# The rope's product with exchanged halves in a hybrid encoder layer: one GpSimd instruction over 512 columns in place of two over 256

## The chip, the cores and the metric

The kernel runs on one core of a Trainium2 chip. The metric is the device time of one launch in microseconds (us), the median of several runs. Instructions go to five engines, each of which works through its own queue in order: TensorE (PE), VectorE (DVE), ScalarE (ACT), GpSimd (POOL) and SyncE (SP, which here issues nearly all DMAs). PEld is TensorE's weight load, which overlaps its products.

## What is computed

One encoder layer on 2048 + 512 tokens of width 1024. The input is normalised and multiplied by a 1024 x 9216 matrix. Some of the columns feed a neighbourhood attention, some feed three groups of dilated sliding-window attention (8 heads of 64 each), and the rest are gates. The change lies in the dilated part, where each query and key head is normalised and rotated:

```python
def rope(x):
    ...
    x1, x2 = xf[..., : dh // 2], xf[..., dh // 2:]
    return jnp.concatenate([x1 * cos - x2 * sin, x2 * cos + x1 * sin], axis=-1).astype(x.dtype)

    for gi, (win, dil) in enumerate(DIL_GROUPS):
        q = rope(rms_norm(heads(parts[base]), qn_b))
        k = rope(rms_norm(heads(parts[base + 1]), kn_b))
        o, lse = dilated_attention(q, k, heads(parts[base + 2]), win, dil)
```

So each output element is its own input times a cosine plus the input of the other half of its head times a signed sine.

## The kernel before, in words

The kernel has four stages, in this order: the dilated projections and attention (`dil_sweeps`, about 40 to 1220 us of the trace), the neighbourhood attention (`na_sweeps`, to about 1800 us), the gates (`gate_sweeps`) and the output product (`out_sweep`). Every value is kept as a sum of two fp16 numbers, "hi" and "lo", and a product is three matmuls.

In the dilated stage there are 60 tiles of 128 tokens (20 for each of the three groups), and each has three projection banks q, k and v of 512 columns: 24 matmuls into one of four PSUM banks named `proj`. For q and k, `dil_qk` (line 1407) does the rest, 120 times in all. ACT copies the bank into a buffer `qk` (there are three) and gives the bank back to PE, then squares it into `sq`; DVE sums the squares by head into `q_ssq`; POOL rotates (`rope`, lines 1433 to 1446): the product with the exchanged halves into `sq` (lines 1437 to 1439, two instructions, one for each half of the heads), the product with the own half in place (line 1441), and the sum of both (line 1442). Beside that, `rsqrt` (line 686) makes the 8 scales `q_y` of each row: two small ACT instructions, and five small POOL instructions on 8 columns (`q_c`, `q_t`, `q_y`). When both are there, POOL multiplies by `q_y` (`scale`, line 1448), ACT rounds to fp16 (`qs`, `high`), DVE or POOL makes the rest (`low`, line 1459), and SP issues the transposing DMAs. The factors `gcs` are made on POOL once for each tile (`rope_gains`, line 1389): for q and for k 64 cosines and 64 signed sines for each row, each times a gain.

The order of the instructions in each engine's queue is not left to the hardware or a compiler. The builder runs a clock of its own (`Clock`, line 112): each helper (`act`, `vec`, `pool`, `dma`) emits its instruction and adds a price to the time at which its engine is free; what follows is put on a heap at the time at which the clock says that the instruction is done, and is emitted when that time is reached. PE's matmuls are emitted as that clock goes on. `either` (line 384) puts an instruction on DVE or on POOL, whichever the clock says is done first. The prices of POOL and of that choice are:

```python
    def pool(self, ins, /, out, *a, n=None, **kw):
        getattr(self.nc.gpsimd, ins)(out, *a, **kw)
        self.clk.run("P", 0.23 + (n or size(out)) / 480)
...
        if self.clk.first(V=0.15 + n / 960 + PORT, P=0.23 + n / 480) == "V":
```

`size` counts the columns of one partition, and `PORT` is 0.18. The buffers (`Slots`) are given out by the same clock. An instruction emitted too early for its data holds up all that stands behind it on its engine.

Of the kernel before, what the change touches and what calls it, by code (L numbers as in the profile page):

```python
# [18 lines left out]
ALU = mybir.AluOpType  # L19
# [248 lines left out]
class Enc:  # L268
# [1138 lines left out]
    def dil_qk(self, R, i, ps):  # L1407

        clk, S, H = self.clk, self.S, R["H"]
        B = {}  # L1410

        def copy():
            B["x"] = self.new("qk", [128, 512])
            self.act(B["x"], ps)
            S["proj"].give(ps)
            S["sq"].take(square)

        def square():
            B["sq"] = self.new("sq", [128, 512])
            self.act(B["sq"], B["x"], AF.Square)  # L1420
            clk.then(reduce)

        def reduce():
            name = f"q{S['qk'].index(B['x'])}"
            ssq = self.T.tile([128, 8], F32, name=f"{name}_ssq", bufs=1)
            self.vec("tensor_reduce", ssq, B["sq"].rearrange("p (h d) -> p h d", d=64), axis=AX.X, op=ALU.add, n=512)
            both = B["both"] = Gate(clk, 2)
            both.when(scale)
            H["cs_gate"].when(rope)
            inv = self.inv["qk"[i], 2 + R["gi"]]  # L1430
            self.rsqrt(B, ssq, 8, QP ** 2 / 64, inv[:, 0:1], inv[:, 1:2], self.lnq, QS * QP, name, both.signal)

        def rope():
            x, sq, gcs = B["x"], B["sq"], H["gcs"]
            x4 = x.rearrange("p (h s e) -> p h s e", s=2, e=32)
            b4 = sq.rearrange("p (h s e) -> p h s e", s=2, e=32)
            for s in range(2):
                self.pool("tensor_tensor", b4[:, :, s], x4[:, :, 1 - s],
                          gcs[:, i, 1, 32 * s:32 * s + 32].unsqueeze(1).to_broadcast([128, 8, 32]), op=ALU.mult)
            x3 = x.rearrange("p (h d) -> p h d", d=64)  # L1440
            self.pool("tensor_tensor", x3, x3, gcs[:, i, 0].unsqueeze(1).to_broadcast([128, 8, 64]), op=ALU.mult)
            self.pool("tensor_tensor", x, x, sq, op=ALU.add)
            S["sq"].give(sq)
            if i == 1:
                S["cs"].give(H["cs"])
            B["both"].signal()

        def scale():
            x3 = B["x"].rearrange("p (h d) -> p h d", d=64)
            self.pool("tensor_tensor", x3, x3, B["y"].unsqueeze(2).to_broadcast([128, 8, 64]), op=ALU.mult)  # L1450
            clk.then(S["qs"].take, high)

        def high():
            B["qs"] = self.new("qs", [128, 1024], FP16)
            B["parts"] = self.parts(B["x"], B["qs"], 8)
            self.act(*B["parts"][0])
            clk.then(low)

        def low():
            self.either("tensor_tensor", *B["parts"][1], op=ALU.subtract)  # L1460
            S["qk"].give(B["x"])
            clk.then(R["place", i].when, turn)

        def turn():
            for out, rows in R["to", i]():
                self.turn(out, B["qs"][rows])
            S["qs"].give(B["qs"])
            R["ch"]["done"][R["i"]].signal()

        S["qk"].take(copy)  # L1470
# [744 lines left out]
```

## Time and profile before

| | |
|---|---|
| median of 3 runs | 2845.07 us (2841.5 to 2846.61) |
| the profiled execution's own time | 2850.0 us |
| its span, first to last instruction | 2847.9 us |
| PE busy | 2653.4 us (93%), 20853 instructions |
| DVE busy | 1612.5 us (57%) |
| ACT busy | 1365.8 us (48%) |
| POOL busy | 1460.0 us (51%) |
| the 16 DMA engines | mean 147 GB/s |

Busy time is the time in which an engine had an instruction under way. Matmuls are pipelined and their ends are modelled, so a busy PE is not PE at its peak; a gap of PE is a gap. PEclk is the clock that was granted to TensorE, as a part of full speed. A wait is put down to the instruction that ended last before it. In the rows, L356 is the helper of all matmuls, L360 that of the small transposes, L364 that of ACT, L369 that of DVE and L381 that of POOL, so instructions are told apart by the names of their tiles, output before inputs.

### The profile page before, as it was taken

To read this page: it belongs to the slowest core of one execution; us is meant where nothing else is said; L and a number is where in the kernel's file an instruction comes from. 1 tells how busy PE (TensorE), PEld (TensorE's weight loads), DVE (VectorE), ACT (ScalarE), POOL (GpSimd) and SP (SyncE) were. 2 spreads that over 40 slices of the span, in tenths; PEclk is the share of its full clock that TensorE was granted. 3 is DMA by queue.
4 is the path that set the end of the run, shared out by engine and by line. 5 is a ranking of instruction groups with operands and counts; after the bars stand their busy time and mean duration, and the time that the engine had idled before them with its cause. 6 is when DMAs were issued, how large, how long until landed. Compare 5 with 4: busy or idle time off the path is not lost. (4 is left out here: it accounts for less than half of the span.)

```text
span 2847.9 us, 55994 instructions
## 1 busy us (share of the span) xinstructions
PE 2653.4 (93%) x20853; PEld 1751.4 (61%) x20853; DVE 1612.5 (57%) x3716; ACT 1365.8 (48%) x3574; POOL 1460.0 (51%) x1996
## 2 busy tenths in 40 slices
PE   5998999989999999999899967799999999999999
PEld 2444444444444444455455544688888888888887
DVE  6787676785655765446686777432264544453111
ACT  5667666666666665656665667321132211222110
POOL 4887778777778898857665764100011221231110
PEclk9999999999999999999999975799999999999999
DMA  7898896776675765578998898431253444453443
GB/s 220 211 202 184 195 192 120 147 137 114 114 128 111 158 115 118 102 205 188 201 226 189 184 196 168 95 82 50 67 163 98 130 131 126 123 189 103 149 144 111
DMA packets 806721, 419.21 MB, mean 147 GB/s; under 512 B 688704, under 2 KB 733056, under 8 KB 800048
## 3 DMA queue, kind: packets, MB, share of 16 engines
q1 hardware_dynamic: 806016, 414.86, 63.4%
q8 instruction: 163, 2.67, 0.4%
q0 software_dynamic: 432, 0.77, 0.2%
q14 instruction: 110, 0.90, 0.1%
HBM read 171.72 MB, written 79.13 MB: 88 GB/s over the span
## 5 line engine op out<-in xcount | busy, mean ns | idle before, releaser
L356 PEld LDWEIGHTS <-hb 128*128 128x128 f16 x6240 | 590.3, 99 | 665.8 <-issue 109.2
L356 PE MATMUL proj<-wt,hb 128*128 128x512 f16 (+2 forms) x3420 | 691.4, 355 | 28.4 <-ACT qk L364 14.3
L356 PE MATMUL proj<-wu,hb 128*128 128x512 f16 x2880 | 663.3, 383 | 34.0 <-ACT qk L364 23.7
L356 PEld LDWEIGHTS <-wt 128*128 128x128 f16 x4560 | 445.8, 98 | 66.7 <-DMA hb<-htd 7.6
L364 ACT ACTIVATE sg<-proj,wi 128x256 f32<-128x256 f32 x240 | 113.0, 473 | 618.2 <-PE proj L356 615.6
L364 ACT ACTIVATE e<-e,neg,sc 128x256 f32<-128x256 f32 (+4 forms) x688 | 393.0, 572 | 5.1 <-DVE neg L369 2.9
L356 PE MATMUL proj<-hb,wt 128*128 128x256 f16 x2760 | 313.8, 273 | 9.8 <-DMA hb<-htd 7.4
L356 PEld LDWEIGHTS <-pT 128*128 128x128 f16 (+1 forms) x4560 | 227.4, 102 | 140.6 <-DMA pT<-p 65.3
L369 DVE TENSOR_TENSOR p<-e,p 128x512 f16<-128x512 f32 (+2 forms) x283 | 249.7, 883 | 65.6 <-ACT p L364 61.9
L381 POOL TENSOR_TENSOR sq<-qk,gcs 128x256 f32<-128x256 f32 x240 | 195.3, 834 | 164.3 <-DVE q_ssq L369 160.2
L381 POOL TENSOR_TENSOR qk<-qk,sq 128x512 f32<-128x512 f32 (+1 forms) x140 | 182.3, 1302 | 188.9 <-DVE qk L369 129.5
L369 DVE SCALAR_TENSOR_TENSOR qk<-s,binv,sg 128x256 f32<-128x256 f32 x160 | 77.1, 483 | 316.4 <-PE s L356 314.0
L356 PE MATMUL proj<-hb,kT 128*128 128x256 f16 x1920 | 227.5, 275 | 2.8 <-DVE kT L369 2.8
L381 POOL TENSOR_TENSOR hb<-sg,hb 128x256 f16<-128x256 f32 x66 | 53.4, 810 | 324.2 <-ACT hb L364 324.2
L356 PE MATMUL s<-hb,wt 128*128 128x256 f16 x1800 | 209.7, 273 | 2.2 <-DVE qk L369 2.1
L356 PEld LDWEIGHTS <-kT 128*128 128x128 f16 x1920 | 188.6, 99 | 26.6 <-DVE kT L369 3.1
L369 DVE CUSTOM_DVE_ANT_0 e<-s,cmask 128x256 f32<-128x256 f32 (+2 forms) x528 | 153.6, 344 | 64.5 <-PE s L356 53.7
L381 POOL TENSOR_TENSOR qk<-qk,q_y 128x512 f32<-128x512 f32 x160 | 177.4, 1113 | 4.8
L369 DVE CAST p<-e 128x512 f16<-128x512 f32 (+2 forms) x173 | 113.1, 654 | 108.1 <-ACT e L364 98.2
L369 DVE TENSOR_REDUCE q_ssq<-sq 128x8 f32<-128x512 f32 x160 | 108.8, 680 | 111.3 <-ACT sq L364 111.0
L381 POOL TENSOR_TENSOR qk<-qk,gcs 128x512 f32<-128x512 f32 x120 | 163.6, 1363 | 9.4
L369 DVE TENSOR_TENSOR qs<-qk,qs 128x512 f16<-128x512 f32 (+1 forms) x137 | 119.5, 874 | 79.3 <-ACT qs L364 77.0
(189 smaller groups left out, 3749.5 us busy)
## 6 DMA issues: line engine op xcount, KB each, us to landing
hb<-htd SPq DMA_DIRECT2D x40, 1024.0 KB
wr<-in_w_in SPq DMA_DIRECT2D x132, 256.0 KB
obd<-osb SPq DMA_DIRECT2D x50, 264.0 KB
hd<-xs SPq DMA_DIRECT2D x20, 512.0 KB
htd<-hb SPq DMA_DIRECT2D x10, 1024.0 KB
mad<-qk SPq DMA_DIRECT2D x40, 256.0 KB
e<-obd SPq DMA_DIRECT2D x40, 256.0 KB
sq<-mad SPq DMA_DIRECT2D x40, 256.0 KB
```

Of the source, the lines that this page charges most:

```text
L356: self.nc.tensor.matmul(out, a, b, start=start, stop=stop, **kw)
L364: self.nc.scalar.activation(out, x, func, **kw)
L369: getattr(self.nc.vector, ins)(out, *a, **kw)
L381: getattr(self.nc.gpsimd, ins)(out, *a, **kw)
```

## The change

Two instructions, each over 8 heads x 32 columns, become one over 8 heads x 2 halves x 32 columns. The input is read with the two halves of each head in reversed order, the sines are read as 64 columns repeated for 8 heads, and the output is written in order. What is multiplied with what, and where it is written, is the same. As `size(out)` is now 512, the builder's own price for this step is another one too.

```diff
@@ -1434,9 +1434,8 @@
             x, sq, gcs = B["x"], B["sq"], H["gcs"]
             x4 = x.rearrange("p (h s e) -> p h s e", s=2, e=32)
             b4 = sq.rearrange("p (h s e) -> p h s e", s=2, e=32)
-            for s in range(2):
-                self.pool("tensor_tensor", b4[:, :, s], x4[:, :, 1 - s],
-                          gcs[:, i, 1, 32 * s:32 * s + 32].unsqueeze(1).to_broadcast([128, 8, 32]), op=ALU.mult)
+            self.pool("tensor_tensor", b4, x4[:, :, ::-1], gcs[:, i, 1].rearrange("p (s e) -> p s e", s=2).unsqueeze(1)
+                      .to_broadcast([128, 8, 2, 32]), op=ALU.mult)
             x3 = x.rearrange("p (h d) -> p h d", d=64)
             self.pool("tensor_tensor", x3, x3, gcs[:, i, 0].unsqueeze(1).to_broadcast([128, 8, 64]), op=ALU.mult)
             self.pool("tensor_tensor", x, x, sq, op=ALU.add)
```

## Rows read from the trace of the kernel before

**Rows 1.** Busy time by stretch: us, then PE, PEld, DVE, ACT, POOL, clock, DMA.
```profile
40.00:400.00 360.00, 324.86 (x2252) 156.89 (x2251) 269.05 (x566) 238.92 (x603) 283.66 (x381) 0.98 0.86 194
400.00:800.00 400.00, 370.22 (x2835) 182.83 (x2834) 275.29 (x676) 258.35 (x723) 310.31 (x423) 0.98 0.71 132
800.00:1220.00 420.00, 410.71 (x3046) 202.61 (x3044) 244.85 (x693) 271.79 (x814) 352.84 (x501) 1.00 0.64 125
1220.00:1640.00 420.00, 393.65 (x3217) 225.80 (x3218) 284.13 (x676) 261.87 (x691) 271.59 (x434) 0.98 0.90 197
1640.00:1800.00 160.00, 105.88 (x1065) 68.74 (x1064) 117.98 (x291) 108.32 (x274) 78.46 (x81) 0.65 0.88 178
1800.00:2848.00 1048.00, 1036.82 (x8407) 909.67 (x8404) 397.41 (x749) 204.69 (x430) 154.25 (x160) 1.00 0.39 117
```

**Rows 2.** Waits, 40 to 1220 us: us in total, times, longest us.
```profile
PE proj L356 <- ACT qk L364: 40.5, 34, 3.2
...
PE proj L360 <- ACT qk L364: 4.2, 2, 2.2
...
ACT neg L364 <- DVE osb L369: 174.5, 137, 5.4
ACT qs L364 <- POOL qk L381: 75.2, 45, 6.9
...
POOL sq L381 <- DVE q_ssq L369: 160.2, 60, 17.2
```

**Rows 3.** Timeline of PE and ACT around two stalls: start, us, instruction, idle before.
```profile
175.27 0.63 ACT L364 ACTIVATE qs<-qk 128x512 f16<-128x512 f32 x1 [3.06 <-POOL qk L381]
175.81 0.58 ACT L364 ACTIVATE qk<-proj 128x512 f32<-128x512 f32 x1
176.44 0.81 PE L356 MATMUL proj<-wu,hb 128*128 128x512 f16 x3 [3.22 <-ACT qk L364]
...
825.17 0.63 ACT L364 ACTIVATE qs<-qk 128x512 f16<-128x512 f32 x1 [0.49 <-POOL qk L381]
...
831.00 3.40 PE L356 MATMUL proj<-wt,hb 128*128 128x512 f16 x15 [0.84 <-ACT qk L364]
```

**Rows 4.** POOL groups by shape, whole span: count, busy us, mean ns, idle before.
```profile
L381 POOL TENSOR_TENSOR sq<-qk,gcs 128x256 f32<-128x256 f32 x240 | 195.3, 834 | 164.3 <-DVE q_ssq L369 160.2 <-DVE x_c L369 1.8 <-DVE x_t L369 1.4
...
L381 POOL TENSOR_TENSOR qk<-qk,gcs 128x512 f32<-128x512 f32 x120 | 163.6, 1363 | 9.4
...
L381 POOL TENSOR_TENSOR bm<-G,namask 128x512 f32<-128x512 f32 x48 | 59.4, 1243 | 27.6 <-DVE mx L369 27.4
```

**Rows 5.** Tile gcs: count, duration ns min/median/max.
```profile
L381 POOL TENSOR_TENSOR sq<-qk,gcs x240: 710/727/1715, 44.3 to 1216.7; 128x256 f32<-128x256 f32 x120
L381 POOL TENSOR_TENSOR qk<-qk,gcs x120: 1263/1272/2134, 45.8 to 1217.5; 128x512 f32<-128x512 f32 x120
```

**Rows 6.** Timeline of POOL, one rope with nothing beside it.
```profile
717.11 1.40 POOL L381 TENSOR_TENSOR sq<-qk,gcs 128x256 f32<-128x256 f32 x2
718.59 1.27 POOL L381 TENSOR_TENSOR qk<-qk,gcs 128x512 f32<-128x512 f32 x1
719.94 1.26 POOL L381 TENSOR_TENSOR qk<-qk,sq 128x512 f32<-128x512 f32 x1
```

**Rows 7.** DVE and POOL groups by shape, 40 to 1220 us: count, busy us, mean ns.
```profile
L369 DVE TENSOR_TENSOR p<-e,p 128x512 f16<-128x512 f32 x146 | 137.6, 943 | 23.2 <-ACT p L364 20.8
L369 DVE TENSOR_TENSOR qs<-qk,qs 128x512 f16<-128x512 f32 x91 | 92.6, 1020 | 68.9 <-ACT qs L364 66.8
...
L369 DVE CAST p<-e 128x512 f16<-128x512 f32 x119 | 85.9, 723 | 77.5 <-ACT e L364 77.1
...
L381 POOL TENSOR_TENSOR qs<-qk,qs 128x512 f16<-128x512 f32 x27 | 34.4, 1276 | 9.8 <-ACT qs L364 9.8
...
L381 POOL TENSOR_TENSOR p<-e,p 128x512 f16<-128x512 f32 x18 | 23.5, 1304 | 9.9 <-DVE p L369 6.0 <-ACT p L364 3.9
```

**Rows 8.** Timeline of POOL and DVE from 382 us, and one undisturbed DVE subtraction.
```profile
382.18 1.27 POOL L381 TENSOR_TENSOR qk<-qk,gcs 128x512 f32<-128x512 f32 x1
383.53 1.59 POOL L381 TENSOR_TENSOR qk<-qk,sq 128x512 f32<-128x512 f32 x1
...
383.09 0.91 DVE L369 TENSOR_TENSOR p<-e,p 128x512 f16<-128x512 f32 x1 [0.88 <-ACT p L364]
...
716.39 0.69 DVE L369 TENSOR_TENSOR qs<-qk,qs 128x512 f16<-128x512 f32 x1 [0.38 <-ACT qs L364]
```

## The prediction, made before the changed kernel was run

> **What bounds the kernel now.** I read the busy times by stretch first [rows 1]. All ropes lie between 40 and 1220 us. PE is busy there for 324.9 + 370.2 + 410.7 = 1105.8 of 1180 us: it leaves 74 us idle, 35 and 30 of them before 800 us and 9 after it. POOL is the next fullest engine, 946.8 us or 80%, and 84% after 800 us, where PE hardly waits: a full POOL alone does not stop PE. After 1800 us PE is busy for 1037 of 1048 us and no rope is left. So a shorter rope can win at most what PE loses in the first 1220 us, and the waits say what that is [rows 2]: 36 stalls of 44.7 us in all, in which PE wants a projection bank that ACT has not yet copied out. The question is why ACT is late. Its copies stand in one queue with everything else, and ahead of them ACT waited for POOL's scaled `qk` 45 times, 75.2 us, and for DVE's maxima 137 times, 174.5 us [rows 2].
>
> The link can be seen whole [rows 3]. At 175.27 us ACT's rounding `qs` starts after 3.06 us of waiting for POOL's `qk`; the copy stands behind it and starts at 175.81; PE goes on at 176.44 after a stall of 3.22. I went through the 36 stalls in this way. In 11 of them ACT had waited for POOL in the 8 us before PE went on; they hold 16.4 us, the first being this one and the last the one at 831.00 (0.84 us, after a wait of 0.49). The other 25, 28.3 us, stand behind a wait for DVE, for a transfer, or behind ACT's own work.
>
> **The instruction itself.** The edit takes out 240 instructions of 256 columns and puts in 120 of 512. No row shows the new form. In the means two halves cost 2 x 834 = 1668 ns [rows 4]. The nearest row is the next instruction of the same rope: same buffers, same repeated factor, 512 columns, 1363 ns [rows 4]. The reversed read alone doesn't argue for more: the neighbourhood bias reads a tile in reversed order both ways at 1243 ns for 512 columns [rows 4]. I take 1363, so 305 ns a rope, 120 x 0.305 = **36.6 us** of POOL's time. The ends are far apart. By the medians it is 2 x 727 - 1272 = 182 ns or 21.8 us [rows 5]. Where nothing disturbs POOL, the step from the first half to the next instruction is 718.59 - 717.11 = 1.48 us and that of a 512 is 719.94 - 718.59 = 1.35 [rows 6]: only 0.13 a rope, 15.6 us. And as a pattern of three steps, one of them backward, is in no row, it may run as slowly as two halves, so nothing at all, or somewhat more. I take the mean and not the quiet value because the stalls happen where POOL is crowded; the excess over the median is 107 ns for each half but 91 for a 512 [rows 4, 5], as if it were paid by the instruction.
>
> **What of that reaches PE.** Of the 120 ropes 60 began on an idle POOL, which had waited for DVE's sums [rows 2]; there the saving only shortens the way of that tile, and the scale waits for ACT's `q_y` as well. Where POOL has fallen behind, one or two ropes lie between the late start and the `qk` that ACT waits for, so each of the 11 stalls shrinks by 0.31 to 0.61 us: 3.4 to 6.7 us. I take **5 us**; the ends are 0 (quiet value, hidden by the next wait) and 16.4 us (all 11 go). The next thing late is then ACT's wait for DVE, which the edit doesn't touch. In the stages behind 1220 us the edit has no instruction: 0.
>
> **The plan.** The builder prices a rope's first step at 2 x (0.23 + 256/480) = 1.53 us before and 0.23 + 512/480 = 1.30 after, 0.23 less, 27.6 us over 120. All that follows in its clock moves, so instructions change places in all five queues, SP's transposes too, and `either` finds POOL free sooner: by that, up to 27.6/1.297 = 21 more subtractions can pass from DVE (`qs` at 1020 ns) to POOL (1276) [rows 7], which gives back all that POOL won and takes some 21 us from DVE. I cost this at zero in the sum, as neither sign has a row for it, and give it its own cases below.
>
> **The sum.** 2850.0 - 5 = 2845 for the profiled execution, which stood 4.9 above the median; against the median of 2845.07 that is **2840**.
>
> **A rule that speaks against it.** DVE and POOL do hold each other up here. A DVE subtraction of 512 columns takes 0.69 us undisturbed; the one issued at 383.09, while POOL's product of 382.18 to 383.45 ran, took 0.91, and POOL's next, issued at 383.53, took 1.59 where 1.26 is usual [rows 6, 8]. Either waits for the other's whole instruction. The Trainium skill (SBUF — State Buffer, "Who interferes with whom") calls it an exclusive lock of the shared ports, held for the whole instruction, by GpSimd or by a VectorE instruction with two inputs in SBUF or in a two-port mode; by that rule a merged product shuts VectorE out for longer than each half did. Priced from rows: the halves hold 120 x 2 x 0.71 = 170 us, 14% of the stage. Of the 356 `p`, `qs` and cast instructions [rows 7] some 51 arrive in them and wait 0.36 on average; in a merged one they would wait 0.64. That is 51 x 0.28, **14 us more of waiting on DVE** (an estimate).
>
> **The rivals.** (a) *That lock decides.* DVE's maxima and roundings come later, ACT waits longer for them, and PE with it: the 25 other stalls grow. If all 14 us reached PE, the sum would be 2840 + 14 = **2854**. It decides from some 11 us on, as 5 are won elsewhere. For it: 174.5 us of ACT's waiting is for DVE. Against: DVE is idle for 25% of the time before 400 us and 31% from there to 800 [rows 1], and POOL, with fewer instructions, is shut out less often itself.
> (b) *The new order is worse.* Place: ACT's queue before 800 us. Its `qs` is put 0.23 us earlier, and an undisturbed chip delivers only 0.13; the rounding stands ahead of a bank's copy before its data are there, as at 175.27. A stall costs 44.7/36 = 1.24 us [rows 2], so ten more cost 12.4: **2852**. It decides from nine or ten more stalls on.
> (c) *The new order is better.* The same price with the other sign, ten stalls fewer: **2828**.
> (d) *The edit doesn't do what it says on the chip*: the merged instruction takes as long as two halves (1668), or the saving is covered by the waits for DVE's sums and for `q_y`: **2845**.
>
> **How the numbers follow.** The forecast (2833 to 2845) has 0.45; (a) 0.10, (b) 0.20, (c) 0.16, (d) 0.09. The spread of the three runs is 0.18%, so 0.2%, 5.7 us, is about what a measurement of this kernel can tell from no change: faster means below 2839.4, slower above 2850.8. The forecast lies at that bound and gives 0.24 to faster and 0.21 to the same. With (c) faster is 0.40; with (d) the same is 0.30; (a) and (b) make slower 0.30. The range goes from somewhat below (c) to somewhat above (a), 2824 to 2858: all the cases stand in it, and beyond it are larger changes of the order, for which I keep 0.2. As both signs hold much of the chance: the likeliest case's own range is 2833 to 2845.
>
> **What would show it.** Right: 120 instructions `sq<-qk,gcs` of 512 columns at a mean near 1363 ns and a minimum near 1263; POOL busy some 37 us less before 1220 us, unless POOL has more `qs` and `p` subtractions than the 27 and 18 of before [rows 7]; ACT's wait for POOL's `qk` below 75 us; PE's wait for ACT's copies near 40; the dilated stage ending about 5 us sooner, and the stages behind it as long as before. Wrong: a mean near 1668 is (d). DVE's `p` and `qs` with means up by 40 ns or more and more waiting of ACT for DVE is (a). A time that moves by over 10 us with most of the difference in stalls at new places, or behind 1220 us where no rope is, is the order, (b) or (c); it would mean that the price in the plan counts for more than the instruction.

## The result, and the profile after

The changed kernel takes 2873.93 us, median of 3 runs (2872.27 to 2874.89), against 2845.07: a ratio of 1.0103 with a 95% interval of 1.008 to 1.0126. It is slower by 29 us, three times what the worst of the rivals gave (2854) and outside the range.

First where the time went. The busy times by stretch of both kernels, cut 6 us after the start of ACT's last copy of a dilated bank (columns as in [rows 1]); the kernel before:

```profile
40.50:1216.30 1175.80, 1105.28 (x8128) 542.07 (x8126) 787.26 (x1925) 765.43 (x2126) 943.26 (x1300) 0.99 0.73 147
1216.30:2847.90 1631.60, 1536.35 (x12684) 1204.20 (x12684) 800.94 (x1723) 578.03 (x1407) 507.85 (x678) 0.96 0.57 144
```

The kernel after:

```profile
40.60:1240.60 1200.00, 1114.86 (x8115) 545.58 (x8113) 797.45 (x1940) 762.81 (x2118) 923.76 (x1181) 0.98 0.71 144
1240.60:2870.50 1629.90, 1535.63 (x12696) 1203.92 (x12696) 798.35 (x1724) 577.13 (x1403) 502.47 (x672) 0.96 0.57 144
```

The dilated stage is 24.2 us longer, the rest 1.7 us shorter. POOL is busy for 19.5 us less in the longer stage, so it got the relief that was meant. PE is idle for 85.1 us instead of 70.5, 14.6 more, and the same matmuls keep it busy for 9.6 us longer, at a granted clock of 0.98 where it was 0.99.

The instruction does what it says. From the tile view of `gcs` after (count, ns min/median/max), to be read against [rows 5]:

```profile
L381 POOL TENSOR_TENSOR sq<-qk,gcs x120: 1260/1272/2852, 44.4 to 1238.2; 128x512 f32<-128x512 f32 x120
L381 POOL TENSOR_TENSOR qk<-qk,gcs x120: 1265/1278/2339, 45.8 to 1239.5; 128x512 f32<-128x512 f32 x120
```

The reversed pattern costs nothing: its median of 1272 ns is no more than its neighbour's 1278. And the waits after, from 40.6 to 1240.6 us (us in total, times, longest), which answer to [rows 2]:

```profile
PE proj L356 <- ACT qk L364: 47.2, 36, 3.3
PE proj L356 <- DVE dv L369: 9.6, 7, 3.6
PE proj L360 <- DVE dv L369: 4.7, 1, 4.7
...
PE o L356 <- DMA pT<-p: 3.9, 4, 1.4
...
PE proj L360 <- ACT qk L364: 2.6, 2, 2.0
...
ACT neg L364 <- DVE osb L369: 203.4, 142, 9.3
...
ACT qs L364 <- POOL qk L381: 97.0, 48, 7.0
```

The same waits of PE for DVE and for transposes in the kernel before, from 40.5 to 1216.3 us:

```profile
PE proj L356 <- DVE wm L369: 7.3, 5, 1.9
PE proj L356 <- DVE dv L369: 6.3, 4, 3.4
...
PE o L356 <- DMA pT<-p: 0.9, 3, 0.4
```

POOL has less to do, and yet ACT waits longer for its `qk`: 97.0 us instead of 75.2, and 203.4 instead of 174.5 for DVE's maxima. PE's stalls behind ACT's copies have grown by 5.1 us (44.7 to 49.8), those behind DVE's `dv` by 8.0 (6.3 to 14.3), and those behind the transposes of `p` by 3.0. No single engine explains this; it looks like other instructions in front, which the experiments below test. The longest of these waits, in the timeline of the kernel after:

```profile
419.31 5.11 DVE L369 SCALAR_TENSOR_TENSOR wv<-wr,gf,wv 128x512 f16<-128x512 f32 x3
...
424.95 1.26 DVE L369 TENSOR_REDUCE wm<-wr 128x1 f32<-128x512 f32 x2
...
427.42 0.69 DVE L369 TENSOR_REDUCE wm<-wr 128x1 f32<-128x512 f32 x1 [1.21 <-DMA wr<-in_w_in]
...
428.78 0.69 DVE L369 SCALAR_TENSOR_TENSOR dv<-proj,dv 128x512 f16<-128x512 f32 x1 [0.28 <-issue]
429.53 0.37 PE L360 MATMUL proj<-ident,wm 128*1 128x128 f32 x1 [4.75 <-DVE dv L369]
...
432.41 0.30 ACT L364 ACTIVATE neg<-osb,sc 128x2 f32<-128x2 f32 x1 [9.29 <-DVE osb L369]
```

DVE's queue has work on the weights of the next group (`wv`, `wm`), one piece of it waiting for its load, ahead of `dv`, the instruction that gives a bank back. PE stands for 4.75 us, the scores behind it come late, and ACT, with a softmax's `neg` at the head of its queue, for 9.29 (the profile puts the last 1.4 us before DVE's maxima down to a transfer). The clock falls with it, by the windows of the kernel after:

```profile
420.00:440.00 20.00, 12.96 (x114) 6.88 (x113) 14.01 (x33) 9.87 (x25) 10.48 (x13) 0.74 0.77 163
```

PE was busy for 13 of these 20 us, at 0.74 of full speed in the mean, that is, for part of them at the lower of its two levels (1.2 instead of 2.4 GHz). So a stall is paid a second time in the clock.

The delay does not come evenly. Counted by ACT's copies of banks (`qk` and `dv` from `proj`), the kernel after loses 11.1 us on the one before between the 51st copy and the 62nd (394 to 484 us of its trace, where the place above lies), 6.2 us from there to the 111th, and 11.7 us between the 111th and the 131st; outside these it wins 4.8. Each of the three groups of tiles has 60 banks, so the two short stretches lie around the changes from group to group. The second of them, before and after, and in it PE's stalls behind `dv` after (before there are none):

```profile
816.90:939.10 122.20, 120.69 (x937) 60.39 (x936) 68.45 (x200) 80.00 (x239) 100.34 (x148) 1.00 0.66 123
```

```profile
831.50:965.40 133.90, 124.37 (x943) 61.40 (x942) 78.14 (x208) 82.96 (x248) 96.34 (x132) 0.99 0.65 122
```

```profile
PE proj L356 <- DVE dv L369: 5.3, 2, 3.6
```

### The profile page after: what moved, and what is told of

The parts are those of the page before. It is cut to its first block, busy times and chain, and to the rows that moved or that the text cites. A ratio compares the mean times of both kernels' runs of the same rounds, so it can differ in the third digit from the quotient of the medians.

```text
span 2870.5 us, 55899 instructions
## 1 busy us (share of the span) xinstructions
PE 2662.3 (93%) x20853; PEld 1754.6 (61%) x20853; DVE 1620.0 (56%) x3733; ACT 1362.2 (47%) x3562; POOL 1435.1 (50%) x1871
## 5 line engine op out<-in xcount | busy, mean ns | idle before, releaser
L381 POOL TENSOR_TENSOR sq<-qk,gcs 128x512 f32<-128x512 f32 x120 | 170.7, 1422 | 188.3 <-DVE q_ssq L369 182.1
L369 DVE TENSOR_TENSOR qs<-qk,qs 128x512 f16<-128x512 f32 (+1 forms) x147 | 136.2, 929 | 90.0 <-ACT qs L364 82.9
L381 POOL TENSOR_TENSOR qk<-qk,gcs 128x512 f32<-128x512 f32 x120 | 171.3, 1427 | 9.4
```

The source lines that it names most:

```text
L369: getattr(self.nc.vector, ins)(out, *a, **kw)
```

## The experiments

Two theories. **A**: the time is lost in the order of the queues, which the builder's clock makes from the price, and the instruction itself wins a little or nothing. **B**: the longer instruction shuts DVE out, and that makes the kernel slower. The edit changes an instruction and its price at once; two kernels take them apart.

**m_old**: the one instruction, with the order of before.

```diff
-            self.pool("tensor_tensor", b4, x4[:, :, ::-1], gcs[:, i, 1].rearrange("p (s e) -> p s e", s=2).unsqueeze(1)
+            self.nc.gpsimd.tensor_tensor(b4, x4[:, :, ::-1], gcs[:, i, 1].rearrange("p (s e) -> p s e", s=2).unsqueeze(1)
                       .to_broadcast([128, 8, 2, 32]), op=ALU.mult)
+            for _ in range(2):
+                clk.run("P", 0.23 + 256 / 480)
```

> One instruction over 512 columns, but charged in the builder's clock as the two halves were (2 x 0.763 us), so that every engine's queue has the order of the kernel before, instruction for instruction. Theory A (the new order lost the time, the instruction itself wins a little): 2838 to 2844 us, POOL's sq<-qk,gcs near 1.37 to 1.42 us, PE's stalls behind ACT's copies at or below the 44.7 us of before. Theory B (the longer instruction shuts DVE out and delays ACT): 2855 to 2875 us, with DVE's p and qs means up by 40 ns or more.

Measured: 2845.63 us against 2845.77 in the same session, ratio 1.0002 (0.9993 to 1.0012). Neither theory's number: the loss is gone, so B falls, but nothing is won. POOL and DVE groups of m_old, 40 to 1220 us (columns as in [rows 4, 7]), POOL first:

```profile
L381 POOL TENSOR_TENSOR qk<-qk,gcs 128x512 f32<-128x512 f32 x120 | 167.6, 1397 | 9.4
L1437 POOL TENSOR_TENSOR sq<-qk,gcs 128x512 f32<-128x512 f32 x120 | 165.7, 1381 | 179.6 <-DVE q_ssq L369 175.4 <-DVE x_c L369 1.8 <-DVE x_t L369 1.5
...
L369 DVE TENSOR_TENSOR p<-e,p 128x512 f16<-128x512 f32 x146 | 141.0, 966 | 22.3 <-ACT p L364 19.8
L369 DVE TENSOR_TENSOR qs<-qk,qs 128x512 f16<-128x512 f32 x91 | 97.3, 1071 | 63.5 <-ACT qs L364 61.5
```

As all queues stand as before, these compare row by row: the step takes 165.7 us in place of 195.3, so 29.6 are won; its neighbour is 34 ns slower; DVE's `p` is 23 ns and its `qs` 51 ns slower, 146 x 0.023 + 91 x 0.051 = 8 us on DVE. And the waits of m_old, 40 to 1220 us:

```profile
PE proj L356 <- ACT qk L364: 39.5, 33, 4.5
...
PE proj L360 <- ACT qk L364: 4.0, 2, 2.2
...
ACT neg L364 <- DVE osb L369: 184.2, 136, 5.4
...
ACT qs L364 <- POOL qk L381: 67.8, 40, 6.7
```

ACT waits 7.4 us less for POOL and 9.7 us more for DVE; PE's stalls behind ACT's copies go from 44.7 to 43.5. And POOL itself waits 15.2 us longer for DVE's sums, 175.4 us where it was 160.2. So nothing that POOL won reached PE; the trace shows these two ways in which it went, and not how much each counted.

**h_new**: the two halves, with the order of the changed kernel.

```diff
             for s in range(2):
-                self.pool("tensor_tensor", b4[:, :, s], x4[:, :, 1 - s],
+                self.nc.gpsimd.tensor_tensor(b4[:, :, s], x4[:, :, 1 - s],
                           gcs[:, i, 1, 32 * s:32 * s + 32].unsqueeze(1).to_broadcast([128, 8, 32]), op=ALU.mult)
+            clk.run("P", 0.23 + 512 / 480)
```

> Two instructions over 256 columns, charged as the one over 512 (0.23 + 512/480 = 1.297 us in all), so that every queue has the order of the changed kernel. Theory A: as slow as the changed kernel or a few us slower, 2872 to 2882 us. Theory B: about the kernel before, 2842 to 2850 us.

Measured: 2882.21 us, ratio 1.0124 (1.0109 to 1.014). The work is that of the kernel before, two halves included; only the places of instructions in the queues differ, and for some of those that the builder may put on either of two engines, the engine. And 36 us are lost. So A is shown: the order loses the time. In the traces m_old has the sequence of the kernel before and h_new that of the kernel after, instruction by instruction on every engine. In the new order the one instruction is worth some 6 to 8 us (2873.9 against 2882.2; the ratios are 0.0021 apart, 6 us, and their intervals overlap).

Why that order is bad was the next question: because POOL's step is priced too low (*price*), or because it is another order (*luck*)? **h_tick** is the kernel before with each half charged 0.001 us more, **m_mid** the one instruction charged 1.41:

```diff
+                clk.run("P", 0.23 + 256 / 480 + 1e-3)
...
+            clk.run("P", 1.41)
```

> The kernel before with each half charged 0.001 us more in the builder's clock and nothing else: the instructions are the same, but their order differs from about the tenth rope on. Theory A, in its strong form (any change of the order moves the time, by luck): a time that differs from 2845 by more than 6 us either way, between 2830 and 2875. Theory A in its weak form (the lower price makes roundings stand too early): within 5 us of 2845, as 0.002 us a rope puts nothing noticeably earlier. Theory B: within 5 us of 2845.

> One instruction over 512 columns, charged 1.41 us, midway between the 1.527 of the two halves and the 1.297 of the change, and near what it takes on the chip in the mean (1.42). Weak form of theory A: between the two, about 2855 us. Strong form: unrelated to the price, anywhere from 2830 to 2880. Theory B: about 2870, as the changed kernel.

Measured: h_tick 2845.47 us (1.0, 0.9986 to 1.0013), m_mid 2863.04 (1.006, 1.0044 to 1.0076). Both spoke for *price*: another order at the same price costs nothing, and half the cut costs about half.

Four more with the one instruction: charged 1.307 (**m_tick_up**), 1.293 (**m_tick_down**), 1.65 (**m_high**), and as in the change, with 0.23 put on a later step (**m_scale**):

```diff
             self.pool("tensor_tensor", x3, x3, B["y"].unsqueeze(2).to_broadcast([128, 8, 64]), op=ALU.mult)
+            clk.run("P", 0.23)
             clk.then(S["qs"].take, high)
```

> The changed kernel with its one instruction charged 0.01 us more (1.307 instead of 1.297); the order is the changed kernel's up to about 300 us of the run and another one after it. If the price is what counts (a POOL step that is charged too little puts ACT's roundings too early): 2868 to 2878 us, as the changed kernel. If it is luck (each order is a draw of its own): a time that differs from 2874 by more than 8 us, most probably below it, 2840 to 2866.

> The changed kernel with its one instruction charged 0.004 us less (1.293); the order is the changed kernel's up to about 560 us and another one after it. Price: 2868 to 2878 us. Luck: differs from 2874 by more than 8 us, but keeps what the changed kernel had lost by 560 us, about 4 us: 2848 to 2866.

> One instruction over 512 columns charged 1.65 us, 0.12 more than the two halves were. Price: roundings stand later than in the kernel before, so 2835 to 2846 us. Luck: anywhere from 2840 to 2880.

> The changed kernel, with the product by the scale, the last POOL step of each tile's query and key, charged 0.23 us more, so that POOL's work for one rope has the total that it was charged before, at another place. Price: back to 2840 to 2850 us. Luck: anywhere from 2840 to 2880.

Measured: 2871.72 us (1.0088), 2880.6 (1.012), 2851.06 (1.0013, 1.0001 to 1.0026) and **2837.33** (0.9967, 0.9955 to 0.9979). This looked like *price* once more, though the higher price didn't win. m_scale beats both kernels.

Then m_scale was taken apart: **m_later** plans only the rounding 0.23 us later, **m_full** only keeps POOL busy longer, **m_scale2** puts 0.46 in place of 0.23, and **h_scale** has m_scale's order with the two halves.

```diff
-            clk.then(S["qs"].take, high)
+            clk.at(clk.done + 0.23, S["qs"].take, high)
...
             clk.then(S["qs"].take, high)
+            clk.run("P", 0.23)
```

> The changed kernel, with the rounding that follows the scale planned 0.23 us later, while POOL counts as free as early as in the changed kernel. If what hurts is that roundings stand too early in ACT's queue: back to 2837 to 2850 us. If what hurts is that POOL's own queue is planned too full: 2865 to 2880 us, as the changed kernel.

> The changed kernel, with POOL counted as busy for 0.23 us after the scale, while the rounding is planned as early as in the changed kernel. Roundings too early: 2865 to 2880 us. POOL's queue too full: 2837 to 2850 us.

> As the version with the scale charged 0.23 us more (2837.3 us), but 0.46 more. If a more careful price goes on winning: 2828 to 2836 us. If 0.23 had already met what the chip takes, or its last 8 us were the luck of one order: 2838 to 2855 us, as the version with the instruction charged 1.65 us (2851).

> The order of the version with the scale charged 0.23 us more, instruction for instruction, but with the two halves in place of the one instruction. If the instruction itself is worth what it was in the changed kernel's order (2882.2 against 2873.9): 2843 to 2848 us. If it is worth nothing once the order is a good one, as it was in the order of before: 2835 to 2840 us.

Measured: m_later 2878.57 us (1.011), m_full 2863.61 (1.0063), m_scale2 2840.48 (0.9976, 0.9966 to 0.9987), h_scale 2842.63 (0.9988, 0.9979 to 0.9997). Neither part brings m_scale's time, and neither reading of "too early" or "too full" holds alone. The instruction is worth 5 to 6 us in this order (2837.3 against 2842.6; the ratios are 0.0021 apart too, and the two intervals just touch). As the kernels of either pair were measured in different sessions, neither worth is sure to a few us.

So there are three pairs with one order (in the traces h_scale has the sequence of m_scale on every engine too). ACT's waits in the two others, halves first, from 40.5 us to the end of the stage, cut as above; h_new (to be read against the kernel after), then h_scale and m_scale:

```profile
ACT neg L364 <- DVE osb L369: 197.1, 138, 8.1
...
ACT qs L364 <- POOL qk L381: 114.3, 53, 7.3
```

```profile
ACT neg L364 <- DVE osb L369: 174.7, 131, 6.4
...
ACT qs L364 <- POOL qk L381: 94.1, 45, 6.9
```

```profile
ACT neg L364 <- DVE osb L369: 181.0, 133, 6.4
...
ACT qs L364 <- POOL qk L381: 79.5, 43, 6.7
```

With the one instruction ACT waits longer for DVE in all three orders (9.7, 6.3 and 6.3 us) and shorter for POOL (7.4, 17.3 and 14.6 us). Where the second outweighs the first, the instruction wins 5 to 8 us; in the order of before it doesn't, and nothing is won. Each of these is one trace, so that is a sign and no proof.

The last six were to say whether the price counts at all: the low price in one group of tiles alone (**m_g0**, **m_g1**, **m_g2**), and in all groups at 1.07, 1.18 and 1.06 (**m_low**, **m_118**, **m_106**).

```diff
+            clk.run("P", 0.23 + 512 / 480 if R["gi"] == 0 else 2 * (0.23 + 256 / 480))
...
+            clk.run("P", 1.07)
```

> One instruction over 512 columns, charged 1.297 us in the first of the three groups of dilated tiles and 1.527 in the other two. If every rope that is charged too little costs its share (36 us over 120 with the halves, 29 with the one instruction): about 10 us over 2845, so 2852 to 2860. If one stage makes the loss: 2842 to 2850 unless it is this one. By the changed kernel's trace, which is 3.5 us behind at the end of this group: 2846 to 2851.

> The same with 1.297 us in the second group alone. Each its share: 2852 to 2860 us. One stage: by the changed kernel's trace this group lost 15.6 us, so 2858 to 2864.

> The same with 1.297 us in the third group alone. Each its share: 2852 to 2860 us. One stage: the changed kernel's trace lost 5 us in this group, so 2848 to 2853.

> One instruction, charged 1.07 us in all three groups, 0.23 less than the change charges. If the price goes on to count: 2885 to 2910 us. If the loss is a step that the change has already taken: 2865 to 2885 us. If it was luck: 2840 to 2865.

> One instruction charged 1.18 us, between the change's 1.297 (2874 us) and 1.07 (2849). If each price gives an order of its own with a time that the price does not foretell: anywhere from 2837 to 2882, most probably 2845 to 2870. If the loss is a smooth hump of the price between 1.07 and 1.53: 2858 to 2870.

> One instruction charged 1.06 us, 0.01 less than the kernel that took 2849 us; the order differs from that one's from about the sixth bank on. A smooth dependence on the price: 2845 to 2853 us. A draw: more than 8 us away from 2849, with a chance of about two in three by the spread of the orders so far (2837 to 2881).

Measured: m_g0 2868.05 us (1.0078), m_g1 2860.63 (1.0052), m_g2 2848.84 (1.0009, 0.9999 to 1.0019); m_low **2848.55** (1.0012, 1.0002 to 1.0023), m_118 2872.2 (1.0102), m_106 **2882.59** (1.0135, 1.0118 to 1.0152). The groups don't add up as shares: m_g0 alone loses 23 us, and more than half of it behind its group, under the old price: its trace stands 10.5 us behind that of before at the 62nd copy of a bank and 24.6 at the 81st. And *price* falls with the last pair. At 1.07, where it should be worst, the time is almost that of before; 0.01 us below, it is 34 us more. The windows of m_low's and of m_106's dilated stage:

```profile
40.10:1218.10 1178.00, 1110.47 (x8115) 542.32 (x8113) 797.85 (x1929) 765.88 (x2120) 926.75 (x1183) 0.98 0.72 147
```

```profile
41.00:1251.10 1210.10, 1115.22 (x8115) 544.04 (x8112) 792.79 (x1926) 763.02 (x2116) 930.76 (x1190) 0.98 0.69 143
```

Same instruction, same matmuls, each engine's work equal within 1%; PE is idle for 67.5 us in one and 94.9 in the other. With the kernels before and after, that makes 17 different orders of the same work, from 2837 to 2883 us: seven of them at 2837 to 2851, ten at 2861 to 2883, and none between. Neighbours share the first part of the order, as far as their prices give the same one, and can share its loss: in the traces m_tick_up and m_tick_down leave the changed kernel's order at about 410 and 670 us (not 300 and 560, as expected), at 670 us 12 of its 24 us are lost, and both stay within 7 us of it.

## Why the prediction was wrong

**What bounds the kernel** held: the whole difference lies in the dilated stage, in PE's idle time and its clock; behind it nothing moved but 1.7 us.

**The instruction** held nearly: 1381 ns in the same order against 1363 forecast (1422 in the new one, where its neighbour takes 1427), 29.6 us won on POOL against 36.6. Most of the shortfall is the halves' busy time: 195.3 us [rows 4], less than 240 times their mean, 200.2.

**What reaches PE** was mis-sized: 5 us forecast; 0 measured in the order of before (the interval allows -2.0 to +3.4 us of change), 6 to 8 and 5 to 6 in the two other orders where it was tried. The weak step here says that the next thing late, ACT's wait for DVE, is not touched by the edit. It is: m_old lengthens it by 9.7 us. Rival (d) had 2845 for the case that the waits for DVE's sums cover the saving; m_old took 2845.6, and those waits grew by 15.2 us. The prediction also counted PE's stalls behind ACT's copies alone, 44.7 us; another 25 us of PE's idle time before stood behind DVE and transposes, and there most of the growth came.

**The lock** of rival (a) works about as described and sized. DVE's busy time in the stage, which is 787.3 us before and 797.5 after, in m_old, h_new, h_scale and m_scale:

```profile
40.50:1217.80 1177.30, 1106.52 (x8126) 542.06 (x8123) 799.73 (x1926) 764.14 (x2125) 921.70 (x1181) 0.99 0.72 147
```

```profile
40.50:1253.80 1213.30, 1118.75 (x8119) 546.50 (x8116) 784.92 (x1941) 763.27 (x2120) 943.73 (x1301) 0.98 0.71 143
```

```profile
40.50:1214.40 1173.90, 1104.33 (x8111) 541.84 (x8110) 786.95 (x1923) 766.48 (x2124) 945.46 (x1296) 0.99 0.72 147
```

```profile
40.50:1211.60 1171.10, 1108.67 (x8133) 543.81 (x8131) 800.49 (x1927) 765.42 (x2128) 918.60 (x1176) 0.98 0.73 148
```

With the one instruction DVE is busy for 12.5 us longer in the order of before, 12.5 in the new one and 13.5 in m_scale's, where (a) estimated 14. (Its estimate kept 51 arrivals for the merged product; by its own working that product, 152 us in all, meets 46, which gives 11 us.) The wide `qs` grows in all three (by 51, 92 and 85 ns), the wide `p` in the order of before alone, and the cast in the two others. The casts of h_new, the kernel after, h_scale and m_scale:

```profile
L369 DVE CAST p<-e 128x512 f16<-128x512 f32 x112 | 76.1, 680 | 70.5 <-ACT e L364 70.3
```

```profile
L369 DVE CAST p<-e 128x512 f16<-128x512 f32 x112 | 80.9, 723 | 71.3 <-ACT e L364 70.9
```

```profile
L369 DVE CAST p<-e 128x512 f16<-128x512 f32 x115 | 77.0, 670 | 81.2 <-ACT e L364 81.1
```

```profile
L369 DVE CAST p<-e 128x512 f16<-128x512 f32 x115 | 81.2, 706 | 77.0 <-ACT e L364 76.7
```

In the order of before the cast stays at 723 ns, 40 to 1220 us. The trace agrees with the Trainium skill (SBUF — State Buffer, "Who interferes with whom") on the two-input instructions, and in these two orders on its point that casts can contend in their two-port modes. The rows that the prediction read as a wait for the other's whole instruction show less: 0.22 and 0.33 us longer, where 0.36 and 0.47 were left of it. So (a) had the lock right and its effect wrong: it may have taken back part of the gain, in the order of before perhaps all of it, but with the order kept the one instruction never made the kernel slower.

**The plan** is the step that failed: "I cost this at zero in the sum, as neither sign has a row for it". h_new puts it at +36 us. The rivals had the mechanism, (b) "the new order is worse", with 0.20, but sized it at ten stalls behind ACT's copies, 12 us. The place was wrong: those stalls hold 49.8 us after (47.2 in the row above and two of 2.6 in all) and 44.7 before, 5 of the 14.6 us that PE lost by idling. DVE's `dv` has 8.0 and transposes 3.0, while DVE's weights give some back; and the 9.6 us by which PE was busy longer go with the clock. The guess of how `either` would move work was wrong too: in the dilated stage POOL has 21 of the wide `qs` where it had 27, and 24 of the wide `p` where it had 18, so in sum none moved. And the reason given in (b), a rounding planned earlier than the chip delivers, is not enough: m_later plans the rounding 0.23 us later and takes 2878.6, though in one more order of its own.

Could the size have been known? Not from one trace: it shows one order, and the spread of orders is seen only in several. But 0.23 us off 120 steps was known to move every queue, and a range that ended 18 us above the best guess was a choice without a row behind it.

What stays open is which feature of an order makes it good. The trace names places, as the one at 424 us and the stretch from the 111th to the 131st copy: that stretch is longer than before in all ten bad orders, by 2.8 to 14.3 us, and in the six good ones beside that of before from 5.0 us shorter to 4.7 longer. But it was picked after the results, none of the counts above tells a good order from a bad one beforehand, and no run changed one place alone.

## What to carry to other kernels

Where a builder's own clock orders the queues, an edit is two edits, an instruction and a price; charge the new instruction like the old one first, so that the order stays, and measure the instruction by that. The order is then a search of its own: here it spread over 45 us, while the instruction was worth 0 to some 8, and the best of both, one instruction in m_scale's order, took 2837 us, 0.3% less than before. Time won on an engine that shares a port is worth what its partner doesn't give back.

## What was not expected of the hardware

A product on GpSimd that reads runs of 32 columns in backward order of the halves runs at the speed of a plain one (median 1272 ns for 512 columns, 1278 for its neighbour), so two calls of 256 (2 x 727) cost 182 ns more than one. And TensorE's clock adds to a bad order: the same matmuls took 9.6 us more of busy time in the changed kernel, which idled 14.6 us more, and the stretch around its longest wait for DVE ran at 0.74. The clock alone does not mark a bad order, though: m_low's stage ran at 0.98 with PE busy for 1110.5 us too, idled for 67.5, and was only 2.2 us longer than before.
